# A diffusion layer on one core: another order of work in the Fourier units, other queues for two stores, other rates for the modulation

## The chip, the cores and the metric

The kernel runs on one core of one Trainium2 chip. The time is that of the device for one execution, in microseconds; the time of the kernel before is the median of three runs, 1972.7 us (1970.7 to 1973.29). A core has a matrix engine (TensorE, PE in the rows, with its weight loads as PEld), VectorE (DVE), ScalarE (ACT), GpSimd (POOL) and SyncE (SP). SP, ScalarE and GpSimd can issue transfers. Each engine works through its own list of instructions in order; semaphores order the engines among themselves.

## The reference: what is computed

One layer of a hybrid diffusion model over 384 tokens (128 of context, 256 latent), model width 2048, all in float32. With two conditioning vectors (one for context, one for latent tokens):

```
mod = silu(cond) @ w_ada + b_ada          # six vectors: shift, scale, gate, twice
h   = rmsnorm(x) * (1 + sc1) + sh1
q, k, v, g, lr_f, lr_b, fo = split(h @ w_in)
o   = gated linear attention in both directions, rmsnorm per head, * silu(g)
f   = real part of the 2-D DFT of fo (positions x 256 channels, four groups)
merged = g_a * (o @ w_br_gla) + g_b * (f @ w_br_four)      # g = sigmoid(h @ w_gate + b_gate)
x   = x + ga1 * rmsnorm(merged @ w_out)
h   = rmsnorm(x) * (1 + sc2) + sh2
x   = x + ga2 * rmsnorm((silu(h @ w_ffn_gate) * (h @ w_ffn_up)) @ w_ffn_down)
```

The outputs are x for both kinds of tokens and the new attention states.

## The kernel before, in words

Every float32 matrix product is made of three matmuls in a reduced format: a weight tile is split into a high part (`whi`, a cast by ScalarE, L275) and a low part (`wlo`, the difference, by VectorE, L276), the activation likewise, and high x high, low x high and high x low are summed in one bank of PSUM.

The weights come as a stream of granules of 128 x 1024 numbers, 512 KB each, in the order of the list `srcs`. `load` issues a granule from SP into one of two buffers `raw` (in the folded stretch two more), `split` casts and subtracts, `take` hands a pair out, and `grab` takes one and pushes the next one through. So the cast of the next granule is issued on ScalarE while TensorE works with the one before. `settle` runs what `split(hold=True)` put off. `catch_up` runs the work put off at the end of the last unit, such as the reading of its bank.

The stages, with their rough places in the profiled span:

- up to 177 us: v and the low-rank decays, with the first modulation vectors.
- 177 to 195 us: the projections for q and k (`proj` over `qk_order`), and 195 to 446 us the first 25 gate units. Between their halves `side()` pulls the attention (`gl`) and `ada`, a generator which makes the remaining modulation vectors: GpSimd loads a tile `adaw` of 512 KB from two buffers (L674), VectorE accumulates it in two operations (L679), at the end of sixteen TensorE gathers the sums (`pr`, L687), ScalarE copies them (`adev`, L653), and TensorE transposes them (`ptm`, L657). `rate` is the number of such steps per pull; it is counted up, so 0.6 gives six steps in ten pulls.
- 446 to 551 us: the last seven gate units, fourteen halves called turns. Behind each turn stands work for the Fourier branch from the list `after`: `ends` and `parts` fold the activations of a pair of slices, and `f` (h, n) multiplies one folded granule (`across_n`, L1017 and L1018, bank `pfo`). Folded granules are prepared on VectorE by `fold_across` (L248, L249), their low part is subtracted late (L282). Each gate unit's result goes through `gate` to memory (`gates_d`), 32 stores of 192 KB by SP.
- 551 to 690 us: the units `o` (output gate of the attention) and from `o` 2 on, behind each, two units `four`, which multiply the transformed Fourier slices with a granule of `w_br_four` (`pf`, L1205 to L1208), copy and add (L1209, L1210), unfold (L1214, L1215), multiply with the gate (y, L1218) and store y in `four_d` (L1219, SP). The end of an `o` unit is `gcol`: transposes to `pt` (L1165), Silu of the bank (`gs`, L1167), a product (L1168) and a split (L364, L365). Here `side()` pulls `summed`, the generator `ada_gemv`, once behind each half gemm of an `o` unit: GpSimd loads `adaw` (L698, two buffers), TensorE multiplies it in four matmuls per step (`pr`, L700).
- 690 to 775 us: sixteen units `a` (`w_br_gla`) with the last four Fourier units among them. The first two pull `summed` for its tail.
- 775 to 910 us: the output projection, again with `ada` between the halves at a rate of 0.82; then the norms and the FFN to the end.

The order on TensorE, ScalarE, VectorE and GpSimd is that of the program (`manual_schedule`); nothing reorders it. Loads are issued ahead as far as their buffers are free.

Of the kernel before, what the change touches and what calls it, by code (L numbers as in the profile page):

```python
# [107 lines left out]
def tile_step(ctx: ExitStack, tc: tile.TileContext, a, o):  # L108
# [59 lines left out]
    for n in range(8):  # L168
        after[n].append(("ends", n))
        after[n + 1].insert(0, ("parts", n))  # L170
        after[n + 2].insert(0, ("f", 0, n))
    for n in range(8):
        after[10 + n * (turns - 10) // 8].append(("f", 1, n))
    across = set()
    for at, todo in enumerate(after):
        srcs.append(a["w_gate"][GF + at // 2, at % 2])
# [79 lines left out]
    def split(at=None, eng=DVE, hold=False, defer=None):  # L256


        if raws:
            raw, pairs, spare = raws.pop(0)  # L260
            if spare and depth[0] > 2:
                spare_raws.append(spare)
            if pairs == 2:
                fold_across(raw)
            while low_due:
                low_due.pop()()
            hi, lo = (
                p.tile([P, G], F32R, tag=t, name=n, bufs=b)
                for n, (p, t, b) in zip(("whi", "wlo"), at or ((wp, "whi", 4), (wp, "wlo", 4)))
            )  # L270
            if pairs == 1:
                raw = fold(raw)

            def rest():
                ACT.copy(hi, raw)  # L275
                sub = lambda: eng.tensor_sub(lo, raw, hi.bitcast(F32))  # L276
                sub() if defer is None else defer.append(sub)
                ready.append((hi, lo))

            if pairs == 2:  # L280
                ACT.copy(hi, raw)
                low_due.append(lambda: (DVE.tensor_sub(lo, raw, hi.bitcast(F32)), ready.append((hi, lo))))  # L282
            elif pairs and hold:
                half_done.append(rest)
            else:
                rest()
# [50 lines left out]
    def proj(pool, x, dst, side=None):  # L337

        p = pool.tile([P, T], F32, tag="mm", name="pmm")
        for g in range(2):  # L340
            gemm(p, grab(), x, 8, k0=8 * g, first=g == 0, last=g == 1)
            while later:
                later.pop()()
            if g:
                later.append(lambda: dst(p))
            step(side)
# [386 lines left out]
    rate = [1.0]  # L733
    ada_gen = ada_rest([(m, half) for m in (2, 3, 4) for half in range(2)][:5])
    ada = paced(ada_gen, rate)
    with ExitStack() as s:
# [191 lines left out]
        def keep(t, i):  # L928
            return lambda p: ACT.copy(t[:, i, :], p)
# [18 lines left out]
        def side():  # L948
            while True:
                next(gl, None)  # L950
                next(ada, None)
                yield

        sd = side()
        for i in qk_order[1:]:
            proj(psm, hT, keep(qk, i), sd)

        def gate(pool, i):
            def dst(p):
                g = pool.tile([P, T], F32, tag="gz", name="gz", bufs=2)  # L960
                ACT.activation(g, p, AF.Identity, bias=bgate[:, i : i + 1])
                SP.dma_start(gates_d[i], g)
            return dst

        for i in range(GF):
# [25 lines left out]
    with ExitStack() as s:  # L991
        more = s.enter_context(tc.tile_pool(name="more", bufs=1))
        hF = [actp.tile([P, 4, 2, T], F32R, tag=t, name="hF") for t in ("C_lo", "B_hi", "B_lo")]
        hF.append(more.tile([P, 4, 2, T], F32R, tag="hF", name="hF"))
        spare_raws.extend([more] * 2)
        depth[0] = 4
        sums, folds = [], {}

        def ends(n):
            t, r = (more.tile([P, 2, T], F32, tag=z, name=z) for z in ("t", "r"))  # L1000
            over_ends(2 * n, t, r)
            over_parts(2 * n, r, False)
            folds[n] = r

        def across_n(h, n):
            if n == 0:
                sums[:] = [pss.tile([P, 2, hi - lo], F32, tag="side", name="pfo") for _ in range(2) for lo, hi, _ in parts]
            w = take()
            push()
            w_of = [x.rearrange("p (g i k c) -> p i k g c", g=2, i=2, k=2) for x in w]  # L1010
            for k in range(2):
                kt = 2 * n + k
                x = hF[kt // 4][:, kt % 4]
                for g in range(2):
                    for i, (lo, hi, _) in enumerate(parts):
                        p = sums[2 * g + i]
                        PE.matmul(p, w_of[0][:, i, k, g, :], x[:, :, lo:hi], start=kt == 0, stop=False)  # L1017
                        PE.matmul(p[:, 0], w_of[1][:, i, k, g, :], x[:, 0, lo:hi], start=False, stop=kt == KT - 1)  # L1018
            if n == 7:
                for g in range(2):  # L1020
                    X.append(px.tile([P, T], F32, tag="yb", name="X", bufs=4))
                    for i, (lo, hi, _) in enumerate(parts):
                        p = sums[2 * g + i]
                        ACT.copy(X[-1][:, lo:hi], p[:, 1])
                        DVE.tensor_add(X[-1][:, lo:hi], X[-1][:, lo:hi], p[:, 0])

        def run_after():
            for at, todo in enumerate(after):
                for what, *n in todo:
                    if what == "ends":  # L1030
                        ends(*n)
                    elif what == "parts":
                        over_parts(2 * n[0], folds.pop(n[0]), True)
                    else:
                        if n == [1, 5]:
                            depth[0] = 2
                            spare_raws.clear()
                        across_n(*n)
                if at == turns // 2:
                    SP.dma_start(cd, a["consts"][:, C_CE:NC])  # L1040
                if at == turns - 1:
                    next(ada, None)
                yield

        ra = run_after()
        for i in range(GF, 32):
            proj(psm, hT, gate(more, i), ra)
        catch_up()
        depth[0] = 0
        xq = px.tile([P, HT], F32, name="xq")  # L1050
        POOL.memset(xq, 0.0)
        qb = pss.tile([P, HT], F32, tag="side", name="pfq")
        for kb in range(0, KT, 4):
            for x_ in range(2):
                for k in range(kb, kb + 4):
                    q = 32 * (k % 4)
                    PE.matmul(
                        qb[q : q + 4, :], wq[:, k, :], hF[k // 4][:, k % 4, x_, 0:HT].bitcast(F32),
                        start=kb == 0 and x_ == 0, stop=kb == KT - 4 and x_ == 1,
                    )  # L1060
        for q in range(0, P, 32):
            ACT.copy(xq[q : q + 4, :], qb[q : q + 4, :])
# [3 lines left out]
    with ExitStack() as s:  # L1066
# [126 lines left out]

        def four(i):

            w = grab(hold=True)
            catch_up()
            d = pm.tile([P, 2, HT], F32, tag="fd", name="fd")
            y = px.tile([P, T], F32, tag="yb", name="y", bufs=4)
            for m, x in enumerate((eT, dT)):  # L1200

                pf = (pss if m else psm).tile([P, 512], F32, tag="side" if m else "mm", name="pf")
                for k in range(4):
                    c = slice(512 * m + k * P, 512 * m + (k + 1) * P)
                    PE.matmul(pf[:, 0 : 2 * HT], w[0][:, c], x[k], start=k == 0, stop=False)  # L1205
                    PE.matmul(pf[:, 0:HT], w[1][:, c], x[k][:, 0:HT], start=False, stop=m == 1 and k == 3)
                if m == 0:
                    PE.matmul(pf[:, 0:HT], wn[0:96, i * P : (i + 1) * P], pnr[0][0:96], start=False, stop=True)  # L1208
                ACT.copy(d[:, m], pf[:, HT : 2 * HT])  # L1209
                DVE.tensor_add(d[:, m], d[:, m], pf[:, 0:HT])  # L1210
            g, _ = gates.pop(("b", i))
            for lo, n, base in ((0, TC, 0), (TC, TL, HC)):
                h = n // 2
                DVE.tensor_add(y[:, lo : lo + h], d[:, 0, base : base + h], d[:, 1, base : base + h])  # L1214
                DVE.tensor_sub(  # L1215
                    y[:, lo + h : lo + n], d[:, 0, base + h : base : -1], d[:, 1, base + h : base : -1],
                )
            DVE.tensor_mul(y, y, g)  # L1218
            SP.dma_start(four_d[i], y)  # L1219
            settle()  # L1220


# [1 line left out]
        for b, i in mix_order:  # L1224
# [12 lines left out]
            else:  # L1237
                catch_up()
                if mT is None:
                    mT = alloc_A()  # L1240
                if i < 2:
                    next(summed, None)
                if KT - 7 <= i < KT - 2:
                    next(ada, None)
# [17 lines left out]
    with ExitStack() as s:  # L1262
# [42 lines left out]
            ACT.activation(sq2, mg32(i), AF.Square)  # L1305
            return sq0, pr, sq2

        rate[0] = 0.82
        spare_h = {-4: ((pe, "hid_hi", 1), (pe, "hid_lo", 1)), -2: ((pe, "S0", 1), (pe, "S1", 1))}
        spare_w = ((adap, "adaw", 2), (adap, "adaw", 2))  # L1310
        raw2 = None
# [739 lines left out]
```

## Time and profile before

| | |
|---|---|
| median of three runs | 1972.7 us (1970.7 to 1973.29) |
| profiled execution | 1976.35 us |
| its span | 1974.5 us |
| mean granted clock of TensorE | 0.994 |
| TensorE busy | 1935.3 us, 98% |
| weight loads | 1699.0 us, 86% |
| VectorE busy | 1637.8 us, 83% |
| ScalarE busy | 914.5 us, 46% |
| GpSimd busy | 85.7 us, 4% |
| DMA | 380.54 MB, 193 GB/s in the mean |

The rows shown in the next parts are of these kinds. A row of waits has the engine, tile and line that waited, what released it, and the time in all, the number of times and the longest. A row of a stretch has its length, then the busy time of PE, PEld, DVE, ACT and POOL with the number of instructions, the mean granted clock of TensorE (1.00 is full speed), the busy share of the DMA engines and GB/s. A row of the timeline has the start, the duration, the engine, the line, the operation, the tiles and, in square brackets, how long the engine had been idle and what ended that.

### The profile page before, as it was taken

How to read it: one execution, taken by the hardware profiler on the slowest of the kernel's cores; microseconds unless marked ns; L12 is line 12 of the kernel's file. 1: busy time of each engine (PE TensorE's matmuls, PEld its weight loads, DVE VectorE, ACT ScalarE, POOL GpSimd, SP SyncE). 2: the span in 40 equal slices, each digit the busy share in tenths (PEclk: the TensorE clock that was granted, in tenths of full speed). 3: DMA queues.
4: the chain of work that ended last, by engine and by line, in shares of the span. 5: the costliest groups of instructions: out<-in, count | busy, mean ns of one | idle time of the engine just before them, and what ended most of it. 6: DMA issues, size and time to landing. Idle time of an engine off the chain costs nothing.

```text
span 1974.5 us, 27637 instructions
## 1 busy us (share of the span) xinstructions
PE 1935.3 (98%) x10566; PEld 1699.0 (86%) x10566; DVE 1637.8 (83%) x2160; ACT 914.5 (46%) x1298; POOL 85.7 (4%) x154
## 2 busy tenths in 40 slices
PE   8998999999999899999999999999999999999997
PEld 5778999999988799999988888888888888888886
DVE  5668898888847688987789998999898989887885
ACT  4234445543555544446454444354444444444444
POOL 0000111110000000004000000000000000000001
PEclk9999999999999999999999999999999999999999
DMA  9976666775657787665335444453636263625243
GB/s 390 384 264 206 237 223 235 244 238 188 193 160 233 251 253 261 213 213 191 129 132 184 146 146 156 159 185 119 194 126 205 99 214 106 205 68 192 79 170 114
DMA packets 200616, 380.54 MB, mean 193 GB/s; under 512 B 14196, under 2 KB 126932, under 8 KB 196132
## 3 DMA queue, kind: packets, MB, share of 16 engines
q1 hardware_dynamic: 186004, 328.12, 48.9%
q0 software_dynamic: 13952, 50.39, 8.3%
q8 instruction: 83, 1.36, 0.3%
q14 instruction: 49, 0.40, 0.1%
q10 hardware_dynamic: 528, 0.26, 0.0%
HBM read 361.94 MB, written 16.78 MB: 192 GB/s over the span
## 4 chain that ended last, share of the span: by engine, by line
PE 80%; DVE 9%; DMA 5%; ACT 3%; issue 3%; SPq 0%; POOL 0%; DVEq 0%; ACTq 0%; POOLq 0%
PE pgu L327 30%; PE pmm L315 21%; PE pdn L327 17%; PE pv L477 3%; DVE adacc L679 2%; DVE wlo L276 1%; DMA raw<-in_w_in 1%; PE pgm L460 1%; PE pmm L1468 1%; PE pf L1205 1%; PE pfo L1017 1%; DMA slab<-in_w_ada 1%; PE ptr L1760 1%; DMA xraw<-in_w_x 1%; ACT whi L275 0%
## 5 line engine op out<-in xcount | busy, mean ns | idle before, releaser
L315 PE MATMUL pmm<-A_hi,whi 128*128 128x384 f32 x1072 | 364.9, 340 | 3.8 <-ACT gs L1167 3.8
L315 PE MATMUL pmm<-A_lo,whi 128*128 128x384 f32 x1072 | 360.9, 337 | 0.0
L315 PE MATMUL pmm<-A_hi,wlo 128*128 128x384 f32 x1072 | 360.4, 336 | 0.0
L1615 ACT CAST whi<-u 128x1024 fp32r<-128x1024 f32 x200 | 210.7, 1054 | 284.1 <-DVE u L1599 86.8
L1615 ACT CAST whi<-raw 128x1024 fp32r<-128x1024 f32 x175 | 184.1, 1052 | 197.8 <-PE pgu L327 59.9
L1626 DVE TENSOR_TENSOR wlo<-u,whi 128x1024 fp32r<-128x1024 f32 x200 | 244.5, 1222 | 32.9 <-ACT whi L1615 18.1
L275 ACT CAST whi<-raw 128x1024 fp32r<-128x1024 f32 x165 | 172.8, 1050 | 193.3 <-DMA raw<-in_w_gate 49.5
L276 DVE TENSOR_TENSOR wlo<-raw,whi 128x1024 fp32r<-128x1024 f32 x163 | 198.8, 1222 | 67.1 <-ACT whi L275 64.1
L327 PE MATMUL pgu<-whi,A_hi 128*128 128x512 f32 x640 | 250.1, 391 | 0.0
L327 PE MATMUL pgu<-whi,A_lo 128*128 128x512 f32 x640 | 249.3, 390 | 0.0
L1626 DVE TENSOR_TENSOR wlo<-raw,whi 128x1024 fp32r<-128x1024 f32 x175 | 213.8, 1222 | 36.0 <-ACT whi L1615 24.8
L315 PEld LDWEIGHTS pmm<-A_hi,whi 128*128 128x128 f32 x1072 | 202.8, 189 | 9.9 <-issue 4.5
L315 PEld LDWEIGHTS pmm<-A_lo,whi 128*128 128x128 f32 x1072 | 203.1, 189 | 0.6 <-DVE A_lo L365 0.5
L315 PEld LDWEIGHTS pmm<-A_hi,wlo 128*128 128x128 f32 x1072 | 202.8, 189 | 0.0
L679 DVE SCALAR_TENSOR_TENSOR adacc<-adaw,spad,adacc 128x1024 f32<-128x1024 f32 x150 | 185.8, 1281 | 1.6 <-DMA adaw<-in_w_ada 1.3
L327 PE MATMUL pdn<-whi,hid_hi 128*128 128x512 f32 x480 | 186.9, 389 | 0.0
L327 PE MATMUL pdn<-whi,hid_lo 128*128 128x512 f32 x480 | 186.8, 389 | 0.0
L327 PE MATMUL pgu<-wlo,A_hi 128*128 128x512 f32 x640 | 184.2, 389 | 0.0
L327 PEld LDWEIGHTS pgu<-whi,A_hi 128*128 128x128 f32 x640 | 120.2, 188 | 26.0 <-issue 0.8
L327 PEld LDWEIGHTS pgu<-wlo,A_hi 128*128 128x128 f32 x640 | 120.2, 188 | 25.3
L327 PEld LDWEIGHTS pgu<-whi,A_lo 128*128 128x128 f32 x640 | 120.2, 188 | 25.0
L327 PE MATMUL pgu<-whi,S 128*128 128x512 f32 x480 | 131.1, 395 | 0.0
(405 smaller groups left out, 3038.0 us busy)
## 6 DMA issues: line engine op xcount, KB each, us to landing
adaw<-in_w_ada POOLq DMA_DIRECT2D x96, 512.0 KB, 4.0
raw<-in_w_d SPq DMA_DIRECT2D x88, 512.0 KB, 3.8
slab<-in_w_ada SPq DMA_DIRECT2D x32, 1024.0 KB, 10.8
raw<-in_w_gate SPq DMA_DIRECT2D x64, 512.0 KB, 4.5
raw<-in_w_g SPq DMA_DIRECT2D x48, 512.0 KB, 3.3
raw<-in_w_u SPq DMA_DIRECT2D x48, 512.0 KB, 3.5
raw<-in_w_in SPq DMA_DIRECT2D x44, 512.0 KB, 4.3
u<-in_w_u SPq DMA_DIRECT2D x40, 512.0 KB, 4.6
```

What stands on the lines that cost most here:

```text
L275: ACT.copy(hi, raw)
L276: sub = lambda: eng.tensor_sub(lo, raw, hi.bitcast(F32))
L315: PE.matmul(dst, w[wi][:, k * n + n0 : k * n + n0 + P], x[xi][:, k0 + k, :], start=first and k == 0 and j == 0, stop=last and k == kts - 1 ...
L327: PE.matmul(dst, stat[x_][m], mov(w[w_], m), start=first and w_ == m == x_ == 0, stop=last and w_ == m == 1,)
L460: PE.matmul(pgv[q : q + 32, :], spad[:, k, :], slab[k // (KT // 2)][:, k % (KT // 2), :], start=k < 4, stop=k >= KT - 4,)
L477: PE.matmul(pv[2 * t + g], hT[x_][:, kb, t * P : (t + 1) * P], w_[:, g * 512 : (g + 1) * 512], start=kb == 0 and j == 0, stop=kb == KT - 1 ...
L679: DVE.scalar_tensor_tensor(acc[:, c, :], w, spad[:, k, c : c + 1], acc[:, c, :], op0=ALU.mult, op1=ALU.add,)
L1017: PE.matmul(p, w_of[0][:, i, k, g, :], x[:, :, lo:hi], start=kt == 0, stop=False)
L1205: PE.matmul(pf[:, 0 : 2 * HT], w[0][:, c], x[k], start=k == 0, stop=False)
L1468: PE.matmul(hp[u], hw[u][j][:, ((k - 1) % 8) * P : ((k - 1) % 8 + 1) * P], h2[m][:, k - 1, :], start=k == 1 and j == m == 0, stop=k == KT ...
L1615: ACT.copy(hi, src)
L1626: DVE.tensor_sub(lo, src, hi.bitcast(F32))
```

## The change

- In the folded stretch, granule (0, n) is multiplied behind turn n + 3 and not n + 2; (1, n) behind turns 11, 11, 11, 12, 12, 13, 13, 13 and not 10, 10, 11, 11, 12, 12, 13, 13.
- In `split` the high part of a granule that is folded or plain is cast at once, also where the rest is put off to `settle`.
- `rate` is 0.6 during the projections of q and k, 1.0 behind them; 0.88 and not 0.82 in the output projection. In the folded stretch `ada` is pulled at the last three turns and not at the last alone.
- The gates are stored by ScalarE's queue, y of the Fourier units by GpSimd's; both were stored by SP.
- `four` calls `catch_up` ahead of `grab`.
- The units `a` pull `summed` at i = 0 and 3 and not at 0 and 1.

```diff
-        after[n + 2].insert(0, ("f", 0, n))
+        after[n + 3].insert(0, ("f", 0, n))
     for n in range(8):
-        after[10 + n * (turns - 10) // 8].append(("f", 1, n))
+        after[turns - 1 - (7 - n) * 2 // 5].append(("f", 1, n))
...
+            if pairs != 2:
+                ACT.copy(hi, raw)
+
             def rest():
-                ACT.copy(hi, raw)
                 sub = lambda: eng.tensor_sub(lo, raw, hi.bitcast(F32))
...
         sd = side()
+        rate[0] = 0.6
         for i in qk_order[1:]:
             proj(psm, hT, keep(qk, i), sd)
+        rate[0] = 1.0
...
                 ACT.activation(g, p, AF.Identity, bias=bgate[:, i : i + 1])
-                SP.dma_start(gates_d[i], g)
+                ACT.dma_start(gates_d[i], g)
...
-                if at == turns - 1:
+                if at >= turns - 3:
                     next(ada, None)
...
         def four(i):
 
+            catch_up()
             w = grab(hold=True)
-            catch_up()
...
             DVE.tensor_mul(y, y, g)
-            SP.dma_start(four_d[i], y)
+            POOL.dma_start(four_d[i], y)
             settle()
...
-                if i < 2:
+                if i in (0, 3):
                     next(summed, None)
...
-        rate[0] = 0.82
+        rate[0] = 0.88
```

## The prediction

> **What bounds the kernel.** I read the page first, then the list of waits of TensorE, then the span cut into stages, then the instructions around each wait. From the page:
>
> ```profile
> PE 1935.3 (98%) x10566; PEld 1699.0 (86%) x10566; DVE 1637.8 (83%) x2160; ACT 914.5 (46%) x1298; POOL 85.7 (4%) x154
> ...
> PE 80%; DVE 9%; DMA 5%; ACT 3%; issue 3%; SPq 0%; POOL 0%; DVEq 0%; ACTq 0%; POOLq 0%
> ```
>
> TensorE is busy for 98% of the span and carries 80% of the chain that ended last. No matmul is removed, so the change can only win idle time of TensorE, or add to it. The 39 us that TensorE is idle are in few places. Its waits (us in total, times, longest) and the stages (PE, PEld, DVE, ACT and POOL busy, then the granted clock):
>
> ```profile
> PE pmm L315 <- ACT gs L1167: 5.8, 4, 2.3
> PE at L854 <- DVE ki L831: 4.6, 1, 4.6
> ...
> PE pfo L1017 <- DVE hF L721: 4.2, 1, 4.2
> PE ptm L657 <- ACT adev L653: 2.8, 2, 2.3
> ```
> ```profile
> 177.00:270.00 93.00, 88.29 (x588) 86.70 (x587) 79.46 (x102) 41.35 (x71) 10.37 (x21) 0.98 0.64 221
> ...
> 447.00:625.00 178.00, 173.33 (x1143) 162.59 (x1142) 130.50 (x207) 85.08 (x142) 10.38 (x20) 0.99 0.61 192
> 625.00:670.00 45.00, 41.23 (x264) 37.63 (x266) 30.07 (x61) 24.99 (x38) 2.32 (x5) 0.96 0.68 221
> 670.00:860.00 190.00, 185.57 (x1094) 182.32 (x1095) 166.68 (x243) 90.85 (x149) 11.60 (x22) 0.99 0.75 248
> 860.00:920.00 60.00, 57.29 (x344) 54.89 (x342) 46.18 (x78) 29.94 (x53) 7.77 (x9) 0.97 0.47 159
> ```
>
> The four waits make 17.4 us, and each part of the change is aimed at one of them. A wait costs more than itself where the clock falls behind it:
>
> ```profile
> 189.10:194.00 4.90, 0.33 (x12) 0.22 (x8) 4.90 (x8) 2.56 (x6) 0.80 (x2) 1.00 0.36 125
> 194.00:198.00 4.00, 4.00 (x33) 3.88 (x34) 4.00 (x7) 0.91 (x1) 0.53 (x1) 0.57 0.58 227
> ...
> 645.20:647.50 2.30, 0.21 (x2) 0.00 (x0) 1.23 (x1) 2.27 (x3) 0.00 (x0) 1.00 0.34 135
> ...
> 645.00:654.00 9.00, 6.72 (x36) 6.01 (x34) 6.85 (x19) 7.16 (x12) 0.00 (x0) 0.81 0.51 157
> 664.00:668.00 4.00, 2.99 (x18) 2.76 (x17) 2.81 (x7) 3.29 (x6) 0.00 (x0) 1.00 0.50 158
> ```
>
> After 4.6 us of idleness the mean clock is 0.57 for 4 us, a loss of 0.43 x 4 = 1.7 us; after 2.1 us near 645 it is 0.81 over 9 us, again 1.7 us; after 1.0 us near 664 it stays 1.00. I price a stall of over 2 us with 1.7 us on top. The Trainium skill (TensorE: Matmul & The Clock Gate, What's actually happening) says that the clock halves after one idle window of about 3.4 us, the windows running freely. By it, a 4.9 us stall would hold a whole window in 44 of 100 cases and one of 6.0 us in 76, so the dips in the sum below would come to 1.7 x (0.44 + 4 x 0.76) = 5.9 us, an estimate, in place of 8.5. The dip after 2.1 us does not agree with it, so the sum keeps the rows.
>
> **Part 1: rate 0.6 in the projections of q and k.** In this stage VectorE holds the exponentials' products back:
>
> ```profile
> 182.30 2.48 DVE L679 SCALAR_TENSOR_TENSOR adacc<-adaw,spad,adacc 128x1024 f32<-128x1024 f32 x2
> ...
> 184.74 1.05 ACT L275 CAST whi<-raw 128x1024 fp32r<-128x1024 f32 x1 [8.12 <-DMA raw<-in_w_in]
> ...
> 189.24 2.48 DVE L679 SCALAR_TENSOR_TENSOR adacc<-adaw,spad,adacc 128x1024 f32<-128x1024 f32 x2
> ...
> 193.24 0.56 DVE L831 TENSOR_TENSOR ki<-ki,qk 128x384 f32<-128x384 f32 x1
> ```
>
> Each step of the modulation (L679) takes 2.48 us of VectorE. The rate cuts its half steps there from 14 to 8.4, and in the changed kernel's order of instructions four of the pairs ahead of L831 are gone, about 4 x 2.48 = 9.9 us of VectorE. That is twice the wait of 4.6 us, so I take 4.6 + 1.7 less a rest of 0.8 = 5.5 us won (ends: 4.6, and 6.3). The pairs aren't lost but run later, with the gates, where TensorE waits for nothing; without slack there, they would come back at 2.48 us each.
>
> **Part 2: folded granules (turn n+3, cast behind the fold) and gate stores by ScalarE.**
>
> ```profile
> 455.48 0.69 DVE L248 TENSOR_TENSOR raw<-raw 128x512 f32<-128x512 f32 x1 [4.13 <-DMA raw<-in_w_in]
> ...
> 460.86 1.23 DVE L276 TENSOR_TENSOR wlo<-raw,whi 128x1024 fp32r<-128x1024 f32 x1 [0.76 <-ACT whi L275]
> 462.01 0.95 DVE L721 TENSOR_TENSOR hF<-r,hF 128x768 fp32r<-128x768 f32 x1
> ...
> gates_d<-gz SPq DMA_DIRECT2D x32, 192.0 KB, 3.7
> ...
> L1916 ACTq DMA_DIRECT2D out_yT<-x1b x1: 417/417/417, 1965.7 to 1965.7; - x1
> ```
>
> VectorE waits 4.13 us for a transfer and then works without a hole to L721, which TensorE awaits for 4.2 us. Half a unit later, one gemm of 4.3 us stands ahead of the first folded matmul, but VectorE gets the sums behind one more subtraction and the later granules are as tight, so most of the win returns in the next turns: 0 to 5.9 us won (4.2 + 1.7), 0.8 taken. The stores cost ScalarE 0.42 us each by its one DMA, behind its own activation, 32 x 0.42 = 13.4 us. ScalarE is busy for 85 of 178 us, so it has the time, but the cast behind the store comes later and VectorE's L276 waited 0.76 us for its cast already: in the seven last gate units 14 halves, every other one with a store, 7 x 0.45 = 3.2 us at worst, 1.8 taken. SP loses 32 issues and its loads go earlier, which nothing here needs. Together +1 us (ends -6 and +4).
>
> **Part 3: emptying the bank first.** The bank is freed by Silu, behind a cast that waits for its transfer:
>
> ```profile
> 644.78 1.05 ACT L275 CAST whi<-raw 128x1024 fp32r<-128x1024 f32 x1 [3.31 <-DMA raw<-in_w_in]
> ...
> 645.85 1.28 ACT L1167 ACT_TABLE_LOAD   x1
> 647.14 0.49 ACT L1167 ACTIVATE gs<-pmm 128x384 f32<-128x384 f32 x1
> ```
>
> With `catch_up()` ahead of `grab` the Silu no longer stands behind that cast, and the four waits of 5.8 us and the dip of 1.7 us behind the longest go. Transposing the modulation's tail an `a` unit later takes away the wait of 2.3 us for L653 near 687 and its dip: 2.3 + 1.7. Together 11.5 us won if nothing else is late there.
>
> **Part 4: y stored by GpSimd.** This decides. GpSimd works in order, and the loads of the modulation's weights (`adaw`) are its other work in this stretch; the last line is their time from issue to landing between 598 and 680 us:
>
> ```profile
> 587.79 0.53 POOL L698 DMA_DIRECT2D adaw<-in_w_ada  x1 [7.61 <-PE pr L700]
> 594.62 0.53 POOL L698 DMA_DIRECT2D adaw<-in_w_ada  x1 [6.29 <-PE pr L700]
> 602.05 0.56 DVE L1218 TENSOR_TENSOR y<-y,gate 128x384 f32<-128x384 f32 x1
> 602.63 0.32 SPq L1219 DMA_DIRECT2D four_d<-y  x1
> 603.72 0.64 PE L700 MATMUL pr<-adaw,spad 128*32 128x256 f32 x8
> 604.69 0.53 POOL L698 DMA_DIRECT2D adaw<-in_w_ada  x1 [9.55 <-PE pr L700]
> 608.68 0.64 PE L700 MATMUL pr<-adaw,spad 128*32 128x256 f32 x8
> 611.13 1.28 ACT L1167 ACT_TABLE_LOAD   x1
> 618.75 0.64 PE L700 MATMUL pr<-adaw,spad 128*32 128x256 f32 x8
> 619.20 0.56 DVE L1218 TENSOR_TENSOR y<-y,gate 128x384 f32<-128x384 f32 x1
> ...
> DMA to landing us min/median/max: 4.6/5.4/6.1
> ```
>
> Two buffers let GpSimd run two steps ahead: what it loads from 587.79 is used at 603.72, 16 us later. In the changed order of GpSimd two stores of `four_d` stand ahead of every two loads from the third `o` unit on, and each store waits for its y (L1218). The load for the next `pr` is then issued only after the second y, its signal (SP's store came 0.02 us behind y) and 0.53 us for the store's own issue, taken as that of a load. `pr` is queued in order on TensorE right behind the first gemm of the next `o` unit, so all matmuls wait with it. For 603.72: y ends at 602.61, the load is issued at 603.2 and lands 5.4 us later, at 608.6: a stall of 4.9 us (4.1 to 5.6 by the shortest and longest landing). For 618.75: y ends at 619.76, landing 625.8, a stall of 7.0 us. There the new Silu comes some 2 us sooner (its table load stood 2.4 us behind `pr`) and a cast of 1.05 us moves ahead of y: y 1 us earlier, 6.0 us. Units 3 to 7 have it: 4.9 + 4 x 6.0 = 28.9 us, and with five dips of 1.7 us, 37.4 us. The second load of each pair follows 0.53 us behind the first and has 5 us more: free. Later, the first load for the accumulation on VectorE (L674) stands behind stores as well: 0 to 2 us, 0.5 taken. SP loses 16 stores for which its loads had to wait; this is a help to part 3.
>
> **Part 5: the rate in the output projection, 0.82 to 0.88, and three pulls in the folded turns.** The modulation's last sums are awaited at the end:
>
> ```profile
> 869.64 2.48 DVE L679 SCALAR_TENSOR_TENSOR adacc<-adaw,spad,adacc 128x1024 f32<-128x1024 f32 x2
> ...
> 873.17 2.48 DVE L679 SCALAR_TENSOR_TENSOR adacc<-adaw,spad,adacc 128x1024 f32<-128x1024 f32 x2
> ...
> 874.51 0.64 PE L687 MATMUL pr<-adacc,selr 128*32 128x256 f32 x8 [0.59 <-DVE adacc L679]
> 875.71 0.64 PE L687 MATMUL pr<-adacc,selr 128*32 128x256 f32 x8 [0.56 <-DVE adacc L679]
> ```
>
> `pr` stands at the same gemm in both kernels, but in the changed order the last pair comes after the four operations of L1292 to L1296 (4 x 0.56 us) and not ahead of them, with nothing saved elsewhere: up to one pair and these, +3 us (0 to 4.7). The pulls at turns 11 to 13 add two pairs to VectorE, 5 us that the 47 idle us of its stage hold.
>
> **Sum.** -5.5 + 1 - 11.5 + 37.4 + 0.5 + 3 = +24.9 us. On the profiled execution (1976.35 us, its span 1974.5) that is 2001.3; it stands 3.65 us above the median of the runs, 1972.7, so on that scale 1997.6, say 1998 us.
>
> **Rivals.** *A, GpSimd's wait is hidden* (the other side): no stall at `pr`. The rest stays: -5.5 + 1 - 11.5 + 0.5 + 3 = -12.5 us, 1960 us. It needs the second y to end 6.0 us ahead of `pr` (0.02 + 0.53 + 5.4), at 597.8 instead of 602.61; at 599.42 its own matmuls have barely ended, since the y chain starts from them. Only if the load had another place on GpSimd could this be. The Trainium skill (Trainium Kernel Development and Optimization, Key Constraints) says that transfers issued from SP, ScalarE and GpSimd share the same 16 DMA engines, and that spreading them only saves issue time; by it the moved stores would be worth next to nothing and the time would be this rival's. No run here shows such a move yet, and the rule leaves out what queues behind a store that waits. *B, small stalls*: shortest landings, y as early as near 602 in all five, and no dips: 5 x 4.1 = 20.5 in place of 37.4, +8 us, 1981 us. For it: the longer TensorE waits, the more VectorE and ScalarE catch up. *C, larger stalls*: the store's 192 KB go through the same queue ahead of the load, and the 7.0 us hold: 4.9 + 4 x 7.0 + 5 x 1.5 + 8.5 = 48.9, +36 us, 2009 us. For it: the pieces of part 3 are busy with DMA (0.74 of the engines near 600 to 650). *D, nothing measurable*: B's stalls with 6 us more won in part 2 and full wins elsewhere, 1973 us.
>
> ```profile
> 600.00:650.00 50.00, 47.24 (x310) 42.80 (x309) 34.50 (x68) 26.94 (x39) 3.17 (x6) 0.98 0.74 237
> ```
>
> **Chances.** Forecast 0.55 (own range 1987 to 2004), B 0.18, C 0.14, A 0.10, D 0.03. The measurement can tell 0.2% (4 us) from no change. Slower 0.87, same 0.03, faster 0.10. The range leaves out A, D and the far end of C: 1977 to 2012.
>
> **What would show it.** Right: a row of waits "PE pr L700 <- DMA adaw" of five times and some 29 us; GpSimd's stores of `four_d` with long idle times ended by y, each pair of loads right behind; no row for L1167 and none of 4 us for L854; five new dips between 600 and 690. Wrong: adaw landing ahead of `pr` (A), L1167 still in the list, or the wait at L1017 as long as before and those of L1018 grown.

## The result, and the profile after

The changed kernel takes 2029.2 us (2028.9 to 2030.7, four runs) against 1973.0 us (1970.7 to 1973.5): the ratio is 1.0289, 95% interval 1.0271 to 1.0307. It is 56 us slower, where 25 us were forecast; the time lies above the range. The profiled execution took 2028.91 us, its span 2027.0.

The page of the changed kernel, busy time and chain:

```profile
PE 1947.3 (96%) x10566; PEld 1706.6 (84%) x10566; DVE 1637.7 (81%) x2160; ACT 916.0 (45%) x1298; POOL 94.9 (5%) x170
...
PE 56%; DVE 9%; issue 8%; DMA 2%; ACT 2%; POOL 1%; ACTq 0%; DVEq 0%; POOLq 0%
```

The instructions are as many as before on TensorE, VectorE and ScalarE; GpSimd has sixteen more, the stores of y. TensorE is idle for 2027.0 - 1947.3 = 80 us, where it was 39. The same matmuls are also busy for 12 us more (1947.3 against 1935.3), at a mean granted clock of 0.981 against 0.994. Its waits in the changed kernel (lines have moved by two to four):

```profile
PE pr L702 <- DMA adaw<-in_w_ada: 40.4, 5, 9.1
PE pmm L317 <- DVE gate L1252: 10.9, 2, 9.1
PE pr L689 <- DVE adacc L681: 6.1, 1, 6.1
PE pfo L1022 <- DVE wlo L284: 4.7, 7, 2.1
```

The row that the prediction named is there, five times, but with 40.4 us and not 29. The waits at L854, at L1167 and the long one of `ptm` are gone. The second and third row are new in their size.

The same matmuls can be found in both traces, so the difference of their starts tells where the time went. The table has it for the last matmul of the attention (L854), the first folded one, the end of the Fourier units behind `o` 2, the last matmul of the last Fourier unit, and the first matmul behind the output projection (L1362); the first row is the kernel before, in us from the start of the span, the others are differences from it. Stretches that are alike in two kernels differ by up to 4 us from one execution to the next, mostly in the attention. The profiled execution of the kernel before is itself 3.4 us above the median of its runs, so most differences of kernels of about its time come out 2 to 5 us lower in the table than in the times.

| kernel | attention | folded | `o` 2 | last Fourier | behind output projection |
|---|---|---|---|---|---|
| before | 398.5 | 463.1 | 599.3 | 738.4 | 907.7 |
| changed | -6.5 | -6.8 | -5.2 | +35.3 | +55.8 |
| y by SP (e1) | -7.1 | -7.4 | -5.7 | -11.2 | -0.2 |
| before, y by GpSimd (e2) | +0.2 | -0.1 | -0.1 | +34.0 | +44.2 |
| loads one step ahead (e3) | -6.6 | -6.8 | -5.3 | -0.6 | +19.3 |
| loads two steps ahead (e12) | -4.6 | -4.9 | -3.5 | -7.6 | +12.5 |
| cast put back (e4) | -5.5 | -5.7 | -4.3 | +28.3 | +48.8 |
| e1 with other rates (e5) | +0.7 | +2.9 | +5.0 | +1.9 | -1.1 |
| e5, cast put back (e8) | -0.4 | +1.7 | +3.8 | -8.5 | -7.8 |
| before, rate 0.6 (e6) | -6.9 | -6.9 | -6.7 | -10.0 | +5.0 |
| before, folded part (e11) | +1.4 | +1.2 | +1.7 | +5.5 | +2.6 |
| before, part 3 (e7) | +3.8 | +4.1 | +4.1 | -7.1 | -2.5 |
| before, gates by ScalarE (e10) | +1.8 | +2.1 | +3.8 | +2.4 | -0.6 |
| part 3, rate 0.8, three pulls (e9) | -3.2 | -3.2 | -3.0 | -15.0 | -15.3 |

In the changed kernel the first three stages are 5 us faster. The `o` and Fourier units cost 40.5 us and the rest up to the norms 20.5 us. One period of the first loss, on GpSimd, TensorE, ScalarE and VectorE of the changed kernel:

```profile
613.86 1.28 ACT L1171 ACT_TABLE_LOAD   x1 [9.85 <-PE pmm L317]
...
621.27 0.55 POOL L1223 DMA_DIRECT2D four_d<-y  x1 [19.84 <-DVE y L1222]
622.26 1.05 ACT L275 CAST whi<-ws 128x1024 fp32r<-128x1024 f32 x1 [2.19 <-DVE ws L237]
623.22 0.54 ACT L1213 COPY fd<-pf 128x194 f32<-128x194 f32 x2
623.57 0.62 DVE L1214 TENSOR_TENSOR fd<-fd,pf 128x194 f32<-128x194 f32 x2 [1.39 <-ACT fd L1213]
625.02 0.56 DVE L1222 TENSOR_TENSOR y<-y,gate 128x384 f32<-128x384 f32 x1
625.88 0.55 POOL L1223 DMA_DIRECT2D four_d<-y  x1 [4.06 <-DVE y L1222]
626.42 1.07 POOL L700 DMA_DIRECT2D adaw<-in_w_ada  x2
632.87 1.08 PE L702 MATMUL pr<-adaw,spad 128*32 128x256 f32 x8 [9.01 <-DMA adaw<-in_w_ada]
```

GpSimd stands for 19.84 us in front of the first store and 4.06 in front of the second, each time for y. Right behind it both loads go out, and TensorE has been idle for 9.01 us when the first lands. Before y there is a second thing to see: ScalarE's copy of `pf` (623.22) stands behind the cast of the folded granule, which waited 2.19 us for VectorE's folding. In the kernel before the order was the other one, and y came sooner behind its matmuls:

```profile
616.30 0.52 ACT L1209 COPY fd<-pf 128x194 f32<-128x194 f32 x2
617.92 1.05 ACT L275 CAST whi<-ws 128x1024 fp32r<-128x1024 f32 x1 [1.10 <-DVE ws L237]
```

Behind each stall the clock is low for longer than before. Rows of stretches of the changed kernel, from the end of each of the five stalls at `pr` to the end of the low clock, and the same for two later waits:

```profile
605.90:612.20 6.30, 6.30 (x25) 5.49 (x26) 0.00 (x0) 0.00 (x0) 0.00 (x0) 0.50 0.46 157
632.90:636.10 3.20, 3.20 (x15) 2.39 (x16) 0.00 (x0) 0.00 (x0) 0.00 (x0) 0.50 0.59 214
657.10:663.40 6.30, 6.28 (x24) 5.46 (x25) 0.03 (x1) 0.00 (x0) 0.00 (x0) 0.50 0.52 191
682.40:687.30 4.90, 4.90 (x20) 4.09 (x21) 0.40 (x1) 0.00 (x0) 0.00 (x0) 0.50 0.75 257
708.80:714.60 5.80, 5.80 (x23) 4.99 (x24) 0.00 (x0) 0.00 (x0) 0.00 (x0) 0.50 0.32 115
797.60:803.40 5.80, 5.79 (x18) 5.80 (x19) 5.77 (x8) 2.24 (x4) 0.53 (x1) 0.50 0.78 266
929.50:936.50 7.00, 6.39 (x30) 4.63 (x31) 2.83 (x6) 1.32 (x2) 0.00 (x0) 0.50 0.55 175
```

The first five make 26.5 us at half clock, a loss of 13.3 us. The two later ones belong to the waits at L1252 and L689. The first of those, in the `a` units:

```profile
784.26 0.54 POOL L1223 DMA_DIRECT2D four_d<-y  x1 [13.75 <-DVE y L1222]
784.79 1.07 POOL L676 DMA_DIRECT2D adaw<-in_w_ada  x2
...
793.38 2.48 DVE L681 SCALAR_TENSOR_TENSOR adacc<-adaw,spad,adacc 128x1024 f32<-128x1024 f32 x2 [9.42 <-DMA adaw<-in_w_ada]
```

The load for VectorE's accumulation goes out behind the last store of y. VectorE waits 9.42 us for it, and behind it in VectorE's order stands L1252, which empties the bank that TensorE needs. In all kernels below that have the stores on GpSimd the longest wait at this line is 7.6 to 9.2 us, in those without it at most 3.7 us.

### The profile page after: what moved, and what is told of

It is laid out like the page before. It is cut to its first block, busy times and chain, and to the rows that moved or that the text cites. A ratio compares the mean times of both kernels' runs of the same rounds, so it can differ in the third digit from the quotient of the medians.

```text
span 2027.0 us, 27593 instructions
## 1 busy us (share of the span) xinstructions
PE 1947.3 (96%) x10566; PEld 1706.6 (84%) x10566; DVE 1637.7 (81%) x2160; ACT 916.0 (45%) x1298; POOL 94.9 (5%) x170
## 4 chain that ended last, share of the span: by engine, by line
PE 56%; DVE 9%; issue 8%; DMA 2%; ACT 2%; POOL 1%; ACTq 0%; DVEq 0%; POOLq 0%
PE pgu L329 29%; PE pdn L329 17%; PE pmm L317 6%; DVE adacc L681 2%; DVE wlo L278 2%; DMA adaw<-in_w_ada 1%; PE pmm L1472 1%; PE pfo L1021 1%; ACT whi L275 1%; PE ptr L1764 1%; DMA raw<-in_w_out 0%; DMA raw<-in_w_d 0%; POOL four_d L1223 0%; PE pfo L1022 0%; DVE t L711 0%
## 6 DMA issues: line engine op xcount, KB each, us to landing
slab<-in_w_ada SPq DMA_DIRECT2D x32, 1024.0 KB, 10.5
```

## The experiments

**e1: y by SP.** The changed kernel with one line back.

```diff
-            POOL.dma_start(four_d[i], y)
+            SP.dma_start(four_d[i], y)
```

> The changed kernel with one line back: y of the Fourier units is stored by SP. Theory (a store on GpSimd's in-order queue holds up the modulation's loads behind it): the five waits of pr for adaw (40.4 us) and the wait of 9.1 us for L1252 in the a units vanish with all their dips of the clock; what is left of the change is -5 us up to the o units, -11 us of waits cured behind them, +6.5 us at the end of the output projection: 1960 to 1970 us. Rival (another part of the change, above all the earlier cast, makes the units late): the waits at pr vanish but waits of the o and a gemms take their place, and the time stays above 1985 us.

Measured: 1974.5 us, ratio to the kernel before 1.0003 (0.9994 to 1.0013). The one line is worth 55 us. All waits at `pr` in the gemv and the long one at L1252 are gone. But the time isn't the 1960 to 1970 us expected: the gain of 11.2 us at the last Fourier unit is lost up to the norms. Its waits:

```profile
PE pr L689 <- DVE adacc L681: 7.9, 1, 7.9
...
PE pf L1210 <- DVE wlo L278: 3.9, 3, 2.3
```

The first is the end of the modulation's accumulation in the output projection, the second a new wait in the Fourier units.

**e2: the kernel before, y by GpSimd alone.** The same line the other way round.

```diff
-            SP.dma_start(four_d[i], y)
+            POOL.dma_start(four_d[i], y)
```

> The kernel before with this one line of the change alone: y is stored by GpSimd. Theory of the queue: five waits of pr for adaw of 6 to 8 us, a wait of about 9 us in the a units, each with some 2.5 to 5 us of lowered clock: +45 to +60 us, 2018 to 2033 us. If the stalls need the other parts too (the later y by the earlier cast), less than half of it: below 2000 us.

Measured: 2018.6 us, 1.0223 (1.0199 to 1.0246), +45.5 us, at the low end of the theory. Its rows:

```profile
PE pr L700 <- DMA adaw<-in_w_ada: 36.6, 5, 8.5
PE pmm L315 <- DVE gate L1248: 8.1, 1, 8.1
```

The stalls don't need the other parts. They are as long as this for a reason of their own: the second y comes sooner than in the changed kernel (GpSimd waits 2.58 us between the two stores of a pair, there some 4.06), but from the issue of the load to the end of the stall 5.6 to 8.2 us pass, 7.1 in the mean, against 5.7 there. Why the loads land later here, no run tells.

**e3 and e12: the loads ahead of the stores.** The changed kernel, y still by GpSimd; only the place of the gemv's loads in the program is another, one step ahead in e3, two in e12.

```diff
-        for k in range(KT):
-            w = adap.tile([P, 1024], F32, tag="adaw", name="adaw", bufs=2)
-            POOL.dma_start(w, a["w_ada"][m - 2, half, k])
+        nxt = fetch(0)
+        for k in range(KT):
+            w = nxt
...
+            if k + 1 < KT:
+                nxt = fetch(k + 1)
             yield
```

(e12 begins with `fetch(0)` and `fetch(1)` and fetches k + 2 at the same place.)

> The changed kernel, y still stored by GpSimd, but ada_gemv issues the load of step k + 1 right behind the matmuls of step k, so that the load for the next o unit stands ahead of the two stores on GpSimd and not behind them. Theory of the queue: the five waits at pr (40.4 us and 12 us of lowered clock) vanish; the wait of 9.1 us in the a units, whose load comes from another generator, stays: 1975 to 1985 us. Rival (GpSimd's transfers are slow as such, or VectorE keeps GpSimd from issuing): the loads still land late and the time stays above 2010 us.

Measured: 1990.1 us, 1.0078 (1.0052 to 1.0104); 39 us of the loss are gone, but 12.1 us of waits at `pr` stay and the time is above the 1975 to 1985 us expected. In the trace of e3:

```profile
599.70 0.54 POOL L1231 DMA_DIRECT2D four_d<-y  x1 [4.01 <-DVE y L1230]
600.24 1.07 POOL L701 DMA_DIRECT2D adaw<-in_w_ada  x2
...
598.40 0.64 PE L708 MATMUL pr<-adaw,spad 128*32 128x256 f32 x8
605.80 0.64 PE L708 MATMUL pr<-adaw,spad 128*32 128x256 f32 x8 [2.37 <-DMA adaw<-in_w_ada]
```

The first `pr` of the unit (598.40) no longer waits, since its load stood ahead of the stores. The load of the second still stands behind them and comes 2.37 us late. That is the queue again, and two steps ahead should end it:

> The changed kernel with y by GpSimd, but the gemv's loads issued two steps ahead in the program: both loads of an o unit stand ahead of the two stores before it. Theory of the queue: the waits at pr that one step ahead left (12.1 us, all at the second pr of a unit) vanish too, and 10 us are won against it; the wait in the a units (7.6 us) stays: 1977 to 1984 us. Rival (GpSimd's stores or loads are slow as such): 1988 us or more.

Measured: 1984.9 us, 1.0062 (1.0043 to 1.0080), at the upper end of what was expected. No wait at `pr` in the gemv is left. The win against e3 was 5 us and not 10 (the two intervals overlap): waits for the low parts (`pf`, 5.0 us) stand in the list that e3 didn't have, and those of the `a` units and of the end stay:

```profile
PE pmm L317 <- DVE gate L1260: 10.7, 2, 8.9
PE pr L689 <- DVE adacc L681: 5.9, 1, 5.9
PE pf L1218 <- DVE wlo L278: 5.0, 4, 2.0
```

So GpSimd's stores and loads aren't slow as such; it was what stood behind a store that waits.

**e4: the cast put back.** The changed kernel with the cast of the folded granule behind `settle`.

```diff
-            if pairs != 2:
-                ACT.copy(hi, raw)
-
             def rest():
+                ACT.copy(hi, raw)
```

> The changed kernel with the cast of the folded granule put back behind settle, all else as changed. If the earlier cast (it waits for the folding on VectorE and stands ahead of the copies of pf on ScalarE) makes y late, the second y comes 1.4 to 2.5 us sooner behind its matmuls and each of the five waits at pr is as much shorter: 28 to 33 us in all in place of 40.4, 2015 to 2023 us. If y is late for another reason: 2027 to 2031 us.

Measured: 2019.1 us, 1.0225 (1.0198 to 1.0252), as expected by the first: 10 us less than the changed kernel, the five waits 31.8 us in place of 40.4.

```profile
PE pr L700 <- DMA adaw<-in_w_ada: 31.8, 5, 7.2
```

**e5 and e8: other rates, and the cast once more.** e1 with the put-off steps made up with the attention; e8 is e5 with the cast put back as in e4.

```diff
-        rate[0] = 1.0
+        rate[0] = 1.08
...
-        rate[0] = 0.88
+        rate[0] = 0.82
```

> The changed kernel with y stored by SP, the rate at 1.08 behind the projections of q and k and at 0.82 in the output projection. The steps of the modulation that the rate of 0.6 puts off are then made up in the stage with the attention, where VectorE is busy for 148 of 177 us, and not drained at the end of the output projection. Theory (the loss of 11 us at that end, in the kernel with y by SP, is the steps put off): the wait at L689 falls from 7.9 to about 2.5 us, and the time to 1961 to 1966 us. Rival (the loss there has another cause): 1972 to 1977 us.

Measured: 1975.5 us, 1.0005 (0.9996 to 1.0015): a miss. The wait at L689 did go, and behind the output projection nothing is lost any more (from +1.9 to -1.1 in the table, where e1 went from -11.2 to -0.2). But the steps cost as much in the attention: 7.8 us between e1 and e5 at its end, 6.7 between e1 and e8, which has the same rates. Some of it may be scatter, but the six kernels with a rate of 0.6 and then 1.0 all end the attention 4.6 to 7.1 us sooner than the kernel before, and these two 0.4 us sooner and 0.7 us later.

> As the run with y by SP and the rates of 1.08 and 0.82, but with the cast of the folded granule put back behind settle. If the early cast is what makes the low parts late at L1210 (3.9 us): those waits go and 2 to 5 us are won against that run, 1957 to 1962 us. If it is worth something there: 1 to 4 us slower than that run.

Measured: 1968.4 us, 0.9973 (0.9959 to 0.9987), 7 us faster than e5: more than the 2 to 5 us expected, from a slower start, so above 1957 to 1962 us. The waits of `pf` for the low parts (3.9 us in e5 as in e1) are gone; the early cast is a loss here also without GpSimd's queue.

**e6: the rate of 0.6 alone.**

```diff
+        rate[0] = 0.6
         for i in qk_order[1:]:
             proj(psm, hT, keep(qk, i), sd)
+        rate[0] = 1.0
```

> The kernel before with the rate of 0.6 in the projections of q and k alone (0.82 in the output projection stays). Theory: the wait of 4.6 us at L854 and its 1.7 us go, -6.5 us; five to six steps of 2.48 us of VectorE come back at the end of the output projection, where VectorE has no room: +10 to +15 us there; in all 1976 to 1983 us. Rival (the steps find room in the gates and the Fourier units): 1966 to 1968 us.

Measured: 1982.1 us, 1.0043 (1.0025 to 1.0062). The attention ends 6.9 us sooner, and the steps come back at the end of the output projection:

```profile
PE pr L687 <- DVE adacc L679: 15.5, 3, 14.8
...
PE at L854 <- DVE ki L831: 0.4, 1, 0.4
```

**e7: part 3 alone.**

```diff
-            w = grab(hold=True)
             catch_up()
+            w = grab(hold=True)
...
-                if i < 2:
+                if i in (0, 3):
```

> The kernel before with part 3 alone: catch_up ahead of grab in four, and the tail of the gemv pulled at units 0 and 3. By the prediction's sum 11.5 us are won: 1960 to 1963 us. If new waits take the place of those for Silu (in the kernel with y by SP, 3.9 us for the low part of the weights at L1210 and 1.6 us at L1252): 1965 to 1969 us.

Measured: 1965.7 us, 0.9966 (0.9952 to 0.9980): 7.3 us won and not 11.5. The waits at L1167 are gone: up to the last Fourier unit its trace wins 11.2 us (from +4.1 to -7.1 in the table). Behind it 4.6 us are lost again (-2.5), and in the `a` units a new wait stands. (The execution shown took 1974.1 us, 8.4 above the median, so the size of this row may differ in others.)

```profile
PE pmm L315 <- DVE gate L1248: 4.6, 3, 3.7
```

**e10 and e11: the other parts alone.** The gates by ScalarE's queue (the one line of the change), and the folded granules later with the early cast (the first two hunks).

> The kernel before with the 32 gates stored by ScalarE's queue and nothing else changed. By the prediction the later casts cost at most 3.2 us and 1.8 were taken: 1972 to 1977 us. If SP's loads that go earlier win more than that: 1967 to 1971 us.

Measured: 1975.8 us, 1.0023 (1.0010 to 1.0036), 3.3 us slower, where the prediction took 1.8.

> The kernel before with the folded granules half a unit later and the cast right behind the folding, stores by SP, catch_up behind grab. By the prediction 0.8 us are won in the folded turns; the earlier cast stands ahead of the copies of pf in the Fourier units and should cost there, as it did with y by SP (7 us between the runs with it and without): 1972 to 1982 us. If the cast costs only together with catch_up ahead of grab: 1970 to 1974 us.

Measured: 1980.0 us, 1.0043 (1.0029 to 1.0057), 7.5 us slower. The waits at L1169, which was L1167, are longer than in the kernel before (5.8 us), and the one wait of 4.2 us at `pfo` has become seven of 3.9 us:

```profile
PE pmm L317 <- ACT gs L1169: 8.3, 4, 2.8
...
PE pfo L1020 <- DVE wlo L284: 3.9, 7, 2.2
```

**e9: what can be kept.** The kernel before with part 3, a rate of 0.8 in the projections of q and k and the pulls at the last three folded turns.

```diff
+        rate[0] = 0.8
         for i in qk_order[1:]:
             proj(psm, hT, keep(qk, i), sd)
+        rate[0] = 1.0
...
-                if at == turns - 1:
+                if at >= turns - 3:
```

> The kernel before with part 3 (bank first, tail at units 0 and 3), a rate of 0.8 in the projections of q and k and the pulls at the last three folded turns; stores by SP. If two to three steps fewer ahead of L831 are enough for the wait of 4.6 us at L854, and the two extra pulls in the turns make them up: L854 below 1.5 us, the wait at L687 below 3 us, 3 to 6 us faster than part 3 alone, 1959 to 1963 us. If every step moved comes back somewhere (VectorE has no room in the units a and the output projection): within 2 us of part 3 alone, 1964 to 1968 us.

Measured: 1962.0 us (1960.8 to 1962.4), 0.9944 (0.9932 to 0.9957): faster than the kernel before by 10.5 us and than the changed one by 67. The wait at L854 fell to 2.1 us and not below 1.5, and L687 is not among the twelve longest waits. Of the 3.7 us won against part 3 alone, no run tells what the rate and what the pulls gave.

## Why the prediction was wrong

The side was right, and so was the mechanism of the five stalls at `pr`; the size was not: +56 us against +25. Four terms of the sum were too small: the five stalls (28.9 us, measured 40.4), the low clock behind them (8.5, measured 13.3), the load for L674 behind the stores (0.5, measured 12) and the end of the output projection (3, measured 9.6). They make 34 us; parts 1 to 3 won some 2 us more than forecast.

- **Part 1 (-5.5 us forecast).** The attention ends 6.5 us sooner, 6.9 in e6. That the steps "run later, with the gates, where TensorE waits for nothing" was wrong: e6 shows them at the end of the output projection, 15.5 us of waits, and e5 and e8 show 7 to 8 us when they run with the attention. VectorE's share of busy time in a stage was taken for room.
- **Part 2 (+1 us).** In the changed kernel +1.3 us from the end of the attention to `o` 2 (-6.5 to -5.2). The wait of 4.2 us at `pfo` came back as seven of 4.7 us, as the text of this part expected. That the early cast has a price in the Fourier units was seen only as 1.05 us: putting it back wins 10 us in e4 and 7 us in e8, and e11, which has it together with the later granules, is 7.5 us slower.
- **Part 3 (-11.5 us).** The waits named did vanish. Alone it won 7.3 us, since 4.6 us are lost behind the last Fourier unit, where a wait at L1248 came. In the changed kernel the stretch cost 40.5 us; less stalls of 40.4 and 13.3 us of low clock, some 13 us were won there.
- **Part 4 (+37.4 us).** The place, the number of stalls and what they wait for came out as worked. Two terms were mis-sized. "y 1 us earlier, 6.0 us": the stalls measured 40.4 / 5 = 8.1 us, because y came later, not sooner. The sum had the second y end with the gemm ahead of `pr`; in the period shown TensorE is idle from 632.87 - 9.01 = 623.86, and y ends at 625.02 + 0.56 = 625.58, 1.7 us behind it: the cast waits for the folding, and the copies of `pf` stand behind the cast. Taking the cast back gives 6.4 us per stall, close to the 5.8 of the sum. The store followed y by 0.30 us and not by 0.02. The landing was about as taken. From the issue of the loads (the rows below) to the ends of the stalls (605.9, 632.9, 657.1, 682.4, 708.8) 4.8 to 6.5 us pass, 5.7 in the mean, where 5.4 stood in the sum. "Five dips of 1.7 us" were 13.3 us and not 8.5.

```profile
600.36 1.07 POOL L700 DMA_DIRECT2D adaw<-in_w_ada  x2
...
651.98 1.07 POOL L700 DMA_DIRECT2D adaw<-in_w_ada  x2
...
677.64 1.07 POOL L700 DMA_DIRECT2D adaw<-in_w_ada  x2
...
702.26 0.54 POOL L700 DMA_DIRECT2D adaw<-in_w_ada  x1
```

- **The load for L674 behind the stores ("0 to 2 us, 0.5 taken").** This is the step that failed for want of working out, and as large an error as the stalls: the wait at L1252 with its low clock. Its price is 9.1 us in the row of waits and 5.8 / 2 = 2.9 us of clock, 12 us. I had applied the rule "what is queued behind the waiting store" to the gemv and not to the other generator whose loads stand in the same queue, and not asked what on VectorE stands behind the late step.
- **Part 5 (+3 us).** The wait is 6.1 us and the low clock behind it 7.0 / 2 = 3.5 us. In e1, where the earlier stages are fast, 11 us are lost up to there. The order of instructions showed one pair in another place; what counts is that VectorE is late by the steps put off in part 1. No run has the rate of 0.88 alone, but it and the three pulls seem to help: the wait is 15.5 us in e6, which has neither, and 7.9 us in e1, which has both.

Of the rivals A is out: no load was hidden. B and D are out too, since the stalls and the dips were longer than in the sum and not shorter. C named larger stalls by the store's own bytes in the queue. The time went its way and beyond, but in the changed kernel, where the loads stand right behind the stores, they landed after 5.7 us in the mean, 0.3 us more than in the sum. In e2 it was 7.1 us, and there C's reason is not excluded. The rule of the Trainium skill beside A, that spreading transfers over issuing engines only saves issue time (Trainium Kernel Development and Optimization, Key Constraints), would have given 1960 us; e2 measured +45.5 us from such a move alone, by what stands behind the store on its engine. The rule that the clock halves after an idle window (the Trainium skill, TensorE: Matmul & The Clock Gate, What's actually happening) gave dips of 5.9 us in the prediction's estimate, for stalls of 4.9 and 6.0 us; with stalls of 7.3 to 9.1 us all five had a dip, and 13.3 us were lost.

## What to carry to other kernels

Before a store is moved to another engine's queue, list what stands behind it there, for every generator that uses the queue: a store waits for its data, and every later load waits with it, however many buffers are free. A prefetch lives from its place in the program as much as from its buffers; with the same loads moved two steps ahead of the stores no wait at `pr` was left (e12). Work that is paced over stages does not vanish when it is slowed in one of them; follow it to where it is drained, and take an engine's share of busy time there for room only if its wait rows say so.

## What the runs showed of the hardware

The low clock comes in pieces of 3.41 us. The kernel before, around the stalls of 2.3 us near 645 and of 2.1 us near 681, then the changed kernel around its first stall at `pr` (598.6 to 605.9):

```profile
644.91:648.32 3.41, 1.13 (x8) 0.90 (x7) 1.84 (x2) 2.70 (x4) 0.00 (x0) 1.00 0.52 144
648.32:651.74 3.42, 3.42 (x12) 3.42 (x12) 2.81 (x9) 3.19 (x7) 0.00 (x0) 0.50 0.36 135
...
679.04:682.45 3.41, 1.75 (x13) 1.52 (x11) 1.23 (x1) 2.47 (x3) 0.00 (x0) 1.00 0.98 312
682.45:685.87 3.42, 3.02 (x17) 3.02 (x18) 2.42 (x8) 2.71 (x6) 0.00 (x0) 1.00 0.93 339
```
```profile
598.57:601.98 3.41, 0.03 (x1) 0.00 (x0) 3.34 (x6) 0.00 (x0) 1.61 (x3) 1.00 0.65 227
601.98:605.40 3.42, 0.00 (x0) 0.00 (x0) 2.31 (x3) 1.99 (x2) 0.00 (x0) 0.50 0.88 262
605.40:608.81 3.41, 2.93 (x14) 2.12 (x15) 0.06 (x1) 0.00 (x0) 0.00 (x0) 0.50 0.91 312
608.81:612.22 3.41, 3.41 (x13) 3.41 (x12) 0.00 (x0) 0.00 (x0) 0.00 (x0) 0.50 0.10 38
```

Near 645 TensorE was busy for 1.13 of 3.41 us, and one piece at half clock followed, 1.7 us lost; near 681 it was busy for 1.75, and none followed. So a whole idle stretch of 3.41 us isn't needed. All fourteen traces, cut so from 180 to 1000 us, have 61 falls of the clock: they came behind pieces in which TensorE was busy for up to 0.52 of the time, but for one of 0.68, and no piece under 0.44 was without.

A longer stall has more pieces. Stalls of 2.3 to 4.6 us in the kernel before had one each, the seven of 6.1 to 9.1 us in the changed kernel three each (10.24 us), and the stalls of 5.3 to 9.2 us in e2 and e4 two or three. A part of them lies in the stall itself; behind its end the seven had 3.2 to 7.0 us at half clock, 1.6 to 3.5 us lost each. The five stalls at `pr`, 8.1 us in the mean, so cost (40.4 + 13.3) / 5 = 10.7 us each.
